# The last 16 attention heads of each layer in pairs: fp32 P times V in the two column halves of TensorE, row sums by adds

## The chip, the cores and the metric

The kernel runs on one core of a Trainium2 chip. Its engines are TensorE (PE; PEld is its weight load), VectorE (DVE), ScalarE (ACT), GpSimd (POOL) and SyncE (SP, which issues nearly all DMAs here). Each takes its own instructions in order, and semaphores hold one engine back until another has done its part. The metric is device microseconds of one execution: before the change 4045.18 us, the median of 3 runs (4043.82 to 4050.78).

## The reference

Two layers of a hybrid block work on 2048 latent tokens behind 256 context tokens, 2304 tokens of width 1024 in all. In each layer a normed and modulated input is projected, and three groups of heads work beside each other: a bidirectional state-space scan (SSD, 6 heads), a bidirectional gated delta rule (GDN, 4 heads) and attention (6 query heads over 2 key-value heads, head width 64). The three outputs are gated, put side by side and projected back. All of it is fp32. For attention the reference does this, in blocks of 128 queries:

```python
q = jnp.moveaxis(q.reshape((Bsz, nb, ATTN_BLOCK) + q.shape[2:]), 1, 0)
s = jnp.einsum('bqhgd,bkhd->bhgqk', qi, k) * scale          # 64 ** -0.5
pr = jax.nn.softmax(s, axis=-1)
o = jnp.einsum('bhgqk,bkhd->bqhgd', pr, v)
```

The latent queries see all 2304 keys; the context queries see the 256 context keys, and only in the first layer.

## The kernel before, in words

A layer goes through three stages: projection of all tokens (lines 370 to 490), then attention together with the SSD and GDN work, and then the output projection (`project`, line 1236).

Attention of the latent tokens is cut into 24 units a layer: 4 blocks of 512 queries times 6 heads. A unit has two parts. `unit_max` (line 521) finds the row maxima: 16 products of 512 keys and 4 of 256 (`pq`, line 536), each reduced by VectorE (`mx`, line 538), and then puts the negated maxima into row 64 of the tile `qm`. `unit_main` (line 550) goes over the 18 tiles of 128 keys (a "key tile" below). For each it makes transposed scores with two products in the fast fp32r form (`pst`, lines 567 and 568), takes the exponential on ScalarE into `pe` (line 570) and accumulates V transposed times P in `po` (line 561). V has a column of ones beside its 64 columns, so `po` has 65 rows, and one of them is the row sum.

In the first 13 units line 561 is one fp32 product of `pe` with `v1`. In the other 11 it is three fp32r products: ScalarE rounds `pe` to `ph` (line 575), VectorE makes the rest `pl` (line 576), V was split once into `vh[0]` and `vh[1]` (lines 658 and 659), and `vh[0]` by `ph`, `vh[1]` by `ph` and `vh[0]` by `pl` are summed in `po`. The function `adv` spreads the maxima of the next unit over the key tiles of this one. PSUM has three score slots (`ps_s`), one `po`, and four more banks, of which SSD has three and attention one (`banks(1, 3)`) until GDN takes all four (`banks(0, 4)`).

Beside these units, and in the same queues of the engines, run in this order: the GDN preparation, the SSD states (line 794: products in the column halves of TensorE, since `bn` has 64 columns a group), the SSD outputs (`ssd_out`, one token tile after the other, `py` in line 861 is its product a tile), and then `gdn_chain`: 36 steps a layer, each needing the state `Sc` of the one before. A step begins with 8 products of line 1105 and ends with line 1132. The chain can begin only when `ssd_out` is through, as it takes over its PSUM banks and its SBUF.

The program is written in this order: GDN preparation, SSD, the first 8 units, `gdn_chain`, the other units. A scheduler then sets each engine's order, with that order and `tc.high_priority()` as priorities; the engines keep to its order at run time.

Of the kernel before, what the change touches and what calls it, by code (L numbers as in the profile page):

```python
# [34 lines left out]
GT = 768  # L35

# [48 lines left out]
def hybrid_kernel(ctx, tc, x, c, ctx_in, c_ctx, norm_w, w_mod, b_mod, w_in, conv_w, conv_b, ssd_A_log,  # L85
# [158 lines left out]
    for l in range(DEPTH):  # L244
# [246 lines left out]
        with ExitStack() as bx:  # L491
            splx = bx.enter_context(ExitStack())
            ap_ = splx.enter_context(tc.tile_pool(reuse_waits="tile", name="ap", bufs=2))
            spl = splx.enter_context(tc.tile_pool(reuse_waits="tile", name="spl", bufs=2))
            vh = []
# [25 lines left out]
            def unit_max(h, q0, qn, k0t, k1t, st):  # L521
                kvh = h // 3
                q2 = ap_.tile([P, 512], F32R, name="q2", bufs=3)
                qm = ap_.tile([65, 512], F32R, name="qm", bufs=3)
# [25 lines left out]
            def unit_main(h, q0, qn, k0t, k1t, st, sp=()):  # L550
# [5 lines left out]
                def pv():  # L556
                    kt, pe, ph, pl = pend.pop(0)
                    vs = slice(kvh * 64, kvh * 64 + 65)
                    ops = [(v1, pe)] if ph is None else [(vh[0], ph), (vh[1], ph), (vh[0], pl)]
                    for j, (v, p) in enumerate(ops):  # L560
                        nc.tensor.matmul(po[0:65, :qn], v[:, kt, vs], p[:, :qn], start=(kt == k0t and j == 0),  # L561
                                         stop=(kt == k1t - 1 and j == len(ops) - 1))

                for kt in range(k0t, k1t):
# [4 lines left out]
                    pe = ap_.tile([P, 512], F32, name="pe", bufs=4)  # L569
                    nc.scalar.activation(out=pe[:, :qn], in_=pt[:, :qn], func=AF.Exp, scale=0.125)  # L570
                    ph = pl = None
                    if kt in sp:
                        ph = spl.tile([P, 512], F32R, name="ph", bufs=2)
                        pl = spl.tile([P, 512], F32R, name="pl", bufs=2)
                        nc.scalar.copy(out=ph, in_=pe)  # L575
                        nc.vector.tensor_tensor(out=pl, in0=pe, in1=ph.bitcast(F32), op=ALU.subtract)  # L576
                    pend.append((kt, pe, ph, pl))
                    if len(pend) > (3 if sp else 1):
                        pv()
# [7 lines left out]
                nc.sync.dma_start(mx_d[640 + h * 64:704 + h * 64, q0:q0 + qn], os_[ob:ob + 64, :qn])  # L587
                yield
# [39 lines left out]
            def attention():  # L628
                big = [(h, LC + qb * 512, 512, 0, NT) for qb in range(LX // 512) for h in range(HQ)]
                small = [] if last else [(h, 0, LC, 0, TC) for h in range(HQ)]  # L630
                sb, ss_ = [{} for _ in big], [{} for _ in small]
                mb = [unit_max(*un, st) for un, st in zip(big, sb)]
# [21 lines left out]
                for i, un in enumerate(big):  # L654
                    if i == 13:
                        for _ in range(2):
                            vh.append(spl.tile([P, NT, 129], F32R, name=f"vh{len(vh)}", bufs=1))
# [651 lines left out]
```

## Time and profile before

| | |
|---|---|
| median of 3 runs | 4045.18 us |
| the profiled execution | 4047.43 us |
| its span, first to last instruction | 4045.6 us |
| mean granted TensorE clock, share of 2.4 GHz | 0.959 |
| TensorE busy (matmuls) | 3760.3 us, 93% |
| VectorE busy | 2682.6 us, 66% |
| ScalarE busy | 1831.1 us, 45% |
| GpSimd busy | 1342.1 us, 33% |

A matmul's time in the profile runs from its start to its modelled end, and consecutive ones overlap; what a matmul costs in a full queue is the distance between the starts. One fp32 matmul of the program stands in the profile as two records, an fp32r one as one record. A row of the windows view gives for each engine the busy time in that stretch and, in brackets, the number of its instructions, then the granted clock, the busy share of the DMA engines and GB/s.

### The profile page before, as it was taken

How to read it: one execution, taken by the hardware profiler on the slowest of the kernel's cores; microseconds unless marked ns; L12 is line 12 of the kernel's file. 1: busy time of each engine (PE TensorE's matmuls, PEld its weight loads, DVE VectorE, ACT ScalarE, POOL GpSimd, SP SyncE). 2: the span in 40 equal slices, each digit the busy share in tenths (PEclk: the TensorE clock that was granted, in tenths of full speed). 3: DMA queues.
4: the chain of work that ended last, by engine and by line, in shares of the span. 5: the costliest groups of instructions: out<-in, count | busy, mean ns of one | idle time of the engine just before them, and what ended most of it. 6: DMA issues, size and time to landing. Idle time of an engine off the chain costs nothing. (4 is left out here: it accounts for less than half of the span.)

```text
span 4045.6 us, 69921 instructions
## 1 busy us (share of the span) xinstructions
PE 3760.3 (93%) x25546; PEld 2839.3 (70%) x25546; DVE 2682.6 (66%) x5114; ACT 1831.1 (45%) x3782; POOL 1342.1 (33%) x1710
## 2 busy tenths in 40 slices
PE   8999999888999988887999999999889999889789
PEld 5899999554566655565678999995545566656567
DVE  7556473787778866665547664747886887666633
ACT  5343342443466655662224433424334566556510
POOL 5112130585267422233303130303762573112300
PEclk9999999999999989987999999999999999988889
DMA  6343432353312444547653434322443224444354
GB/s 201 100 141 111 133 110 92 107 156 136 103 55 64 90 108 107 127 100 235 206 168 112 152 104 136 112 99 79 145 135 105 58 66 96 104 103 114 91 173 153
DMA packets 554115, 484.38 MB, mean 120 GB/s; under 512 B 133992, under 2 KB 488620, under 8 KB 553772
## 3 DMA queue, kind: packets, MB, share of 16 engines
q1 hardware_dynamic: 511916, 444.51, 37.7%
q10 hardware_dynamic: 41856, 35.40, 2.9%
q8 instruction: 202, 3.31, 0.3%
q14 instruction: 141, 1.16, 0.1%
HBM read 335.59 MB, written 144.18 MB: 119 GB/s over the span
## 5 line engine op out<-in xcount | busy, mean ns | idle before, releaser
L570 ACT ACTIVATE pe<-pst 128x512 f32<-128x512 f32 (+1 forms) x876 | 512.0, 594 | 635.8 <-PE pst L568 602.2
L538 DVE TENSOR_REDUCE mx<-pq 128x1 f32<-128x512 f32 (+1 forms) x972 | 590.4, 626 | 134.8 <-PE pq L536 130.1
L561 PE MATMUL po<-pe,v 128*65 128x512 f32 x960 | 492.4, 602 | 3.9 <-ACT os__12072 L584 3.9
L536 PE MATMUL pq<-khh,q 128*128 128x512 f32 (+1 forms) x972 | 455.5, 499 | 29.8 <-DVE mx L538 25.9
L567 PE MATMUL pst<-q,khh 128*128 128x512 f32 (+1 forms) x876 | 437.5, 500 | 38.5 <-DVE mx L538 36.4
L455 PE MATMUL ps<-hi,wh 128*128 128x384 f32 (+2 forms) x1296 | 441.1, 340 | 0.0
L455 PE MATMUL ps<-lo,wh 128*128 128x384 f32 (+2 forms) x1296 | 441.1, 340 | 0.0
L455 PE MATMUL ps<-hi,wl 128*128 128x384 f32 (+2 forms) x1296 | 441.0, 340 | 0.0
L576 DVE TENSOR_TENSOR pl<-pe,ph 128x512 fp32r<-128x512 f32 x396 | 318.7, 809 | 108.7 <-ACT ph L575 68.9
L401 PE MATMUL ps<-wh,hi 128*128 128x320 f32 (+1 forms) x1120 | 354.4, 318 | 1.6 <-DVE hi L365 1.6
L568 PE MATMUL pst<-qm,klo 65*128 65x512 f32 (+1 forms) x876 | 355.1, 407 | 0.0
L401 PE MATMUL ps<-wh,lo 128*128 128x320 f32 (+1 forms) x1120 | 349.8, 315 | 1.7 <-DVE lo L366 1.7
L401 PE MATMUL ps<-wl,hi 128*128 128x320 f32 (+1 forms) x1120 | 350.4, 314 | 0.0
L536 PEld LDWEIGHTS pq<-khh,q 128*128 128x128 f32 x972 | 187.3, 195 | 185.0 <-issue 70.2
L376 DVE TENSOR_TENSOR wl<-wt,wh 128x1024 fp32r<-128x1024 f32 (+3 forms) x144 | 175.3, 1246 | 167.2 <-ACT wh L375 165.0
L567 PEld LDWEIGHTS pst<-q,khh 128*128 128x128 f32 x876 | 171.1, 195 | 156.8 <-DVE mx L538 64.1
L575 ACT CAST ph<-pe 128x512 fp32r<-128x512 f32 x396 | 243.5, 619 | 81.9 <-PE po L561 34.9
L561 PE MATMUL po<-ph,vh 128*65 128x512 f32 x792 | 270.1, 423 | 0.1
L455 PEld LDWEIGHTS ps<-lo,wh 128*128 128x128 f32 x1296 | 244.0, 188 | 10.3
L455 PEld LDWEIGHTS ps<-hi,wl 128*128 128x128 f32 x1296 | 243.4, 188 | 10.4
L455 PEld LDWEIGHTS ps<-hi,wh 128*128 128x128 f32 x1296 | 243.4, 188 | 10.2
L1236 PE MATMUL psd<-woh,mh 128*128 128x512 f32 x544 | 217.4, 400 | 16.4 <-ACT mh L1227 15.1
(587 smaller groups left out, 8086.9 us busy)
## 6 DMA issues: line engine op xcount, KB each, us to landing
wt<-in_w_in_dram SPq DMA_DIRECT2D x72, 512.0 KB
wmt<-in_w_mod_dram SPq DMA_DIRECT2D x48, 512.0 KB
pre_d<-pre SPq DMA_DIRECT2D x34, 512.0 KB
acv<-pre_d SPq DMA_DIRECT2D x34, 512.0 KB
kqc<-kt_d SPq DMA_DIRECT2D x68, 256.0 KB
acv<-pre_d SPq DMA_DIRECT2D x68, 256.0 KB
wt<-in_w_in_dram SPq DMA_DIRECT2D x24, 668.0 KB
wt<-in_w_in_dram SPq DMA_DIRECT2D x24, 640.0 KB
```

Source lines behind the costliest of these rows:

```text
L376: nc.vector.tensor_tensor(out=wl[:, ks, :], in0=wt, in1=wh[:, ks, :].bitcast(F32), op=ALU.subtract)
L401: nc.tensor.matmul(ps, hh[:, k, a], ww[:, k, :], start=(n == 0), stop=(n == 3 * KD - 1))
L455: nc.tensor.matmul(ps, ww[:, k, m * P:(m + 1) * P], hh[:, k, s0:s0 + sn], start=(n == 0), stop=(n == 3 * KD - 1))
L536: nc.tensor.matmul(pq[:, :n], q2[:, u * P:(u + 1) * P], khh[:, kvh, k0t * P + a:k0t * P + a + n], start=True, stop=True)
L538: nc.vector.tensor_reduce(mx[:, u, i:i + 1], pq[:, :n], axis=AX.X, op=ALU.max)
L561: nc.tensor.matmul(po[0:65, :qn], v[:, kt, vs], p[:, :qn], start=(kt == k0t and j == 0), stop=(kt == k1t - 1 and j == len(ops) - 1))
L567: nc.tensor.matmul(pt[:, :qn], khh[:, kvh, ks], q2[:, :qn], start=True, stop=False)
L568: nc.tensor.matmul(pt[:, :qn], klo[:, kvh, ks], qm[:, :qn], start=False, stop=True)
L570: nc.scalar.activation(out=pe[:, :qn], in_=pt[:, :qn], func=AF.Exp, scale=0.125)
L575: nc.scalar.copy(out=ph, in_=pe)
L576: nc.vector.tensor_tensor(out=pl, in0=pe, in1=ph.bitcast(F32), op=ALU.subtract)
L1236: nc.tensor.matmul(ps, a, w[k][:, n * 512:n * 512 + 512], start=(k == 0 and i == 0), stop=(k == KD - 1 and i == 2))
```

## The change

The first 8 units of a layer stay as units of one head with the single fp32 product. The other 16 become 8 pairs of two heads over the same 512 queries. A pair goes over the 18 key tiles; for each it makes the scores of both heads, two exponentials into the two halves of one `pe` of 128 x 2 x 512, and every second key tile a "visit" of TensorE multiplies two key tiles: four fp32 products with 64 columns of V, head 0 into the rows 0 to 63 of `po` and head 1 into the rows 64 to 127. The column of ones is not used in a pair: the row sums come from adding up the `pe` tiles (128 x 1024 in one add), 12 of the 18 key tiles on VectorE (11 adds, `acc[0]`) and 6 on GpSimd (5 adds, `acc[1]`), and four products with ones at the end of the pair (`pl`, line 637 of the changed kernel). The splits of P and V are gone. There are 6 buffers of `pe`, each twice as large, in place of 4.

```diff
@@ unit_main: the split is gone, one product is left @@
-                    kt, pe, ph, pl = pend.pop(0)
-                    vs = slice(kvh * 64, kvh * 64 + 65)
-                    ops = [(v1, pe)] if ph is None else [(vh[0], ph), (vh[1], ph), (vh[0], pl)]
-                    for j, (v, p) in enumerate(ops):
-                        nc.tensor.matmul(po[0:65, :qn], v[:, kt, vs], p[:, :qn], start=(kt == k0t and j == 0),
-                                         stop=(kt == k1t - 1 and j == len(ops) - 1))
+                    kt, pe = pend.pop(0)
+                    nc.tensor.matmul(po[0:65, :qn], v1[:, kt, kvh * 64:kvh * 64 + 65], pe[:, :qn], start=(kt == k0t), stop=(kt == k1t - 1))
...
@@ new: pair_main @@
+                def visit(n, behind_mm):
+                    with tc.high_priority():
+                        for v in range(n):
+                            kt, pe = pend.pop(0)
+                            for j in range(2):
+                                c0 = kvh[j] * 65
+                                mm = nc.tensor.matmul(po[half[j]], v1[:, kt, c0:c0 + 64], pe[:, j], start=(kt == k0t), stop=(kt == k1t - 1))
+                                if v == 0 and j == 0:
+                                    behind(mm, behind_mm)
+
+                for kt in range(k0t, k1t):
+                    ks = slice(kt * P, (kt + 1) * P)
+                    pe = ap_.tile([P, 2, 512], F32, name="pe", bufs=PB)
+                    for j in range(2):
+                        pt = aslot("pst")
+                        nc.tensor.matmul(pt, khh[:, kvh[j], ks], st["q2"][j], start=True, stop=False)
+                        mm = nc.tensor.matmul(pt, klo[:, kvh[j], ks], st["qm"][j], start=False, stop=True)
+                        nc.scalar.activation(out=pe[:, j], in_=pt, func=AF.Exp, scale=0.125)
+                        if j == 0:
+                            yield
+                    e = int((kt - k0t) % 3 == 1)
+                    eng = (nc.vector, nc.gpsimd)[e]
+                    if e in acc:
+                        eng.tensor_tensor(out=acc[e], in0=acc[e], in1=pe, op=ALU.add)
...
+                    pend.append((kt, pe))
+                    if len(pend) == 3:
+                        visit(2, mm)
+                    yield
+                visit(len(pend), mm)
+                os_ = ap_.tile([P, 512], F32, name="os2", bufs=1)
+                nc.scalar.copy(out=os_, in_=po)
+                pl = aslot("pl")
+                for j in range(2):
+                    for e in range(2):
+                        nc.tensor.matmul(pl[half[j]], cc("ones")[:, 0:64], acc[e][:, j], start=(e == 0), stop=(e == 1))
...
@@ attention(): 8 units, then 8 pairs @@
+                units = [(1, un) for un in big[:NS]] + [(2, un) for un in big[NS::2]]
```

What the scheduler makes of it on TensorE, in the first layer while the GDN chain runs. Before, about unit 18 of 24 (L567 and L568 are the scores, L561 the three products with V, L536 the next unit's maxima, L1105 the first products of a chain step):

```order
L536 MATMUL pq<-khh,q_18102 128x512 x2
L567 MATMUL pst<-q_17807,khh 128x512
L568 MATMUL pst<-qm,klo 128x512
L561 MATMUL po<-pl,vh_16904 65x512
L561 MATMUL po<-ph,vh_16904 65x512
L561 MATMUL po<-ph,vh_16905 65x512
L1105 MATMUL p<-Sc,kqc 64x64 x8
```

After, at a like place (L613 and L614 are the scores, L604 a visit, L1159 the first products of a chain step):

```order
L613 MATMUL pst<-q_17173,khh 128x512
L614 MATMUL pst<-qm,klo 128x512
L536 MATMUL pq<-khh,q_17710 128x512 x2
L1159 MATMUL p<-Sc,kqc 64x64 x8
L1168 MATMUL p<-Sc,kqc 64x64 x2
L613 MATMUL pst<-q_17327,khh 128x512
L614 MATMUL pst<-qm,klo 128x512
L604 MATMUL po<-pe,v_352 64x512 x4
```

Three products of 65 columns a key tile and head have become one of 64, and four of them stand together. Counted over the whole order, the first layer's last score product stands behind 33 steps of the chain before and behind 30 after; in the second layer behind 35 and 30. The first SSD output tile stands at about unit 10.1 before and 9.2 after in the first layer, 34.4 and 33.9 (counting on) in the second. The first chain step of the first layer stands at about unit 15.2 before and 14.4 after.

The end of the first layer's second pair on TensorE after the change (L637 are the products of the two sums `acc` with ones, L613 and L614 the first scores of the next pair, the others SSD):

```order
L604 MATMUL po<-pe,v_352 64x512
L915 MATMUL py<-xn_10157,m_10161 128x64 x3
L637 MATMUL pl<-acc_16474,cst 64x512
L613 MATMUL pst<-q_16423,khh 128x512
L614 MATMUL pst<-qm,klo 128x512
L901 MATMUL po_10286<-S,bc 128x192
L902 MATMUL po_10286<-S,bc 128x192
L637 MATMUL pl<-acc_16520,cst 64x512
```

The first `acc` is VectorE's, the second GpSimd's; the products that wait for them stand in front of SSD products and of the next pair's.

VectorE in the second layer's SSD outputs after the change (L624 and L621 are the adds, L538 the maxima, L898 to L904 SSD):

```order
L899 TENSOR_TENSOR m_29511<-m_29511,ee 128x384
L624 TENSOR_TENSOR acc_36068<-pe 128x1024
L922 TENSOR_SCALAR t_29426<-t_29426,sq 128x384
L904 TENSOR_TENSOR t_29519<-po_29543,ecum 128x192
L904 TENSOR_TENSOR t_29520<-po_29543,ecum 128x192
L538 TENSOR_REDUCE mx<-pq 128x1 x2
L904 TENSOR_TENSOR t_29519<-po_29568,ecum 128x192
```

The adds stand between SSD's work and the maxima, in a part of the program where before the single fp32 product asked nothing of VectorE.

## Rows read from the trace of the kernel before

**Rows 1.** The page's first part: busy us, share of the span, instructions.

```profile
PE 3760.3 (93%) x25546; PEld 2839.3 (70%) x25546; DVE 2682.6 (66%) x5114; ACT 1831.1 (45%) x3782; POOL 1342.1 (33%) x1710
```

**Rows 2.** Windows: stretch, its us, PE, PEld, DVE, ACT, POOL busy, clock, DMA, GB/s.

```profile
1051.00:1126.70 75.70, 74.14 (x316) 40.19 (x315) 60.41 (x117) 36.95 (x82) 20.98 (x22) 1.00 0.25 78
1126.70:1396.40 269.70, 258.44 (x1217) 166.64 (x1216) 223.57 (x440) 180.79 (x466) 168.94 (x180) 0.99 0.27 69
1396.40:1809.40 413.00, 362.45 (x4722) 248.46 (x4721) 271.66 (x462) 246.80 (x476) 104.38 (x88) 0.90 0.48 111
3162.40:3400.00 237.60, 226.68 (x1051) 145.89 (x1051) 193.28 (x381) 153.28 (x398) 145.71 (x157) 0.97 0.25 64
3400.00:3819.70 419.70, 372.61 (x4713) 255.03 (x4713) 278.96 (x467) 253.46 (x489) 100.14 (x86) 0.91 0.47 108
```

**Rows 3.** Windows of line 1105 alone (PE, PEld): 16 records are one chain step.

```profile
1396.40:1809.40 413.00, 27.09 (x528) 21.97 (x528) 0.90 0.48 111
3400.00:3819.70 419.70, 26.91 (x544) 21.79 (x544) 0.91 0.47 108
```

**Rows 4.** Windows of line 567 alone: 18 records are one unit.

```profile
1126.70:1396.40 269.70, 49.11 (x94) 17.72 (x94) 0.99 0.27 69
```

**Rows 5.** Timeline of TensorE, fp32r products in a row: start us, us, engine, line.

```profile
1702.15 0.39 PE L567 MATMUL pst<-q,khh 128*128 128x512 f32 x1
1702.38 0.39 PE L568 MATMUL pst<-qm,klo 65*128 65x512 f32 x1
```

**Rows 6.** Timeline of TensorE, one fp32 product with V, then SSD products in column halves.

```profile
1034.93 1.02 PE L561 MATMUL po<-pe,v 128*65 128x512 f32 x2
1035.39 0.79 PE L536 MATMUL pq<-khh,q 128*128 128x512 f32 x1
1036.02 0.39 PE L567 MATMUL pst<-q,khh 128*128 128x512 f32 x1
1036.25 0.39 PE L568 MATMUL pst<-qm,klo 65*128 65x512 f32 x1
1036.57 0.55 PE L794 MATMUL pst<-xd,bn 128*64 128x192 f32 x4
1037.05 0.66 PE L781 MATMUL pt<-cst,xb 128*128 128x128 f32 x4
```

**Rows 7.** Line 794, all its records: ns min/median/max, first and last start.

```profile
L794 PE MATMUL pst<-xd,bn x288: 326/326/377, 1015.9 to 3121.6; 128*64 128x192 f32 x144
```

**Rows 8.** Two SBUF operands: ns min/median/max; of L376 busy us, mean ns.

```profile
L217 DVE TENSOR_TENSOR wml<-wmt,wmh x24: 1202/2074/3407, 6.7 to 2014.9; 128x1024 fp32r<-128x1024 f32 x24
L217 POOL TENSOR_TENSOR wml<-wmt,wmh x24: 2352/2518/8822, 8.2 to 2013.9; 128x1024 fp32r<-128x1024 f32 x24
L821 DVE SCALAR_TENSOR_TENSOR m<-cst,sp,m x204: 334/342/1114, 1117.4 to 3353.4; 128x128 f32<-128x128 f32 x102
L845 DVE TENSOR_TENSOR m<-m,ee x68: 541/788/1385, 1125.2 to 3374.2; 128x384 f32<-128x384 f32 x68
L376 DVE TENSOR_TENSOR wl<-wt,wh 128x1024 fp32r<-128x1024 f32 x72 | 88.3, 1251 | 77.8 <-ACT wh L375 75.6 <-DMA q<-qt_d 2.2
```

**Rows 9.** VectorE's groups from 1126.7 to 1396.4: busy, mean ns, idle before.

```profile
L821 DVE SCALAR_TENSOR_TENSOR m<-cst,sp,m 128x128 f32<-128x128 f32 x96 | 47.3, 555 | 0.9 <-POOL m L818 0.9
L576 DVE TENSOR_TENSOR pl<-pe,ph 128x512 fp32r<-128x512 f32 x39 | 33.4, 863 | 5.0 <-ACT ph L575 4.9
```

**Rows 10.** TensorE's waits from 1396.4 to 1809.4: us in total, times, longest.

```profile
PE po L561 <- DVE pl L576: 10.0, 3, 3.7
PE pq L536 <- DVE mx L538: 8.6, 4, 2.7
```

**Rows 11.** Timeline of TensorE, the last chain steps of the first layer.

```profile
1809.48 0.68 PE L1105 MATMUL p<-Sc,kqc 64*64 64x64 f32 x16
1815.32 0.68 PE L1105 MATMUL p<-Sc,kqc 64*64 64x64 f32 x16
1819.40 0.68 PE L1105 MATMUL p<-Sc,kqc 64*64 64x64 f32 x16 [0.61 <-DVE Sc L1132]
```

More of the change, by code (lines that the diff above doesn't have):

```diff
@@ L35 @@
 GT = 768
+PB = 6
+NS = 8
 def rev(t):
@@ L587, in unit_main, with pair_max @@
                 nc.sync.dma_start(mx_d[640 + h * 64:704 + h * 64, q0:q0 + qn], os_[ob:ob + 64, :qn])
+                yield
+            def pair_max(h0, q0, qn, k0t, k1t, st):
+                st.update(q2=[], qm=[])
+                gens = []
+                for j in range(2):
+                    sj = {}
+                    g = unit_max(h0 + j, q0, qn, k0t, k1t, sj)
+                    for i, _ in enumerate(g):
+                        if i == 0:
+                            st["q2"].append(sj["q2"])
+                            st["qm"].append(sj["qm"])
+                        yield
@@ L630, in attention @@
                 small = [] if last else [(h, 0, LC, 0, TC) for h in range(HQ)]
-                sb, ss_ = [{} for _ in big], [{} for _ in small]
-                mb = [unit_max(*un, st) for un, st in zip(big, sb)]
+                units = [(1, un) for un in big[:NS]] + [(2, un) for un in big[NS::2]]
+                sb, ss_ = [{} for _ in units], [{} for _ in small]
+                mb = [(unit_max if n == 1 else pair_max)(*un, st) for (n, un), st in zip(units, sb)]
                 ms = [unit_max(*un, st) for un, st in zip(small, ss_)]
@@ L653, in attention @@
                         pass
[L654 to L657, printed above, removed]
-                        nc.scalar.copy(out=vh[0], in_=v1)
-                        nc.vector.tensor_tensor(out=vh[1], in0=v1, in1=vh[0].bitcast(F32), op=ALU.subtract)
-                    spn = () if i < 13 else range(NT)
+                at = 0
+                for i, (n, un) in enumerate(units):
                     nxt = ms[i:i + 1] + mb[i + 1:i + 2]
-                    left = (21 + 3) * (i + 1 < len(big)) + 3 * (i < len(small))
+                    left = (24 * units[i + 1][0] if i + 1 < len(units) else 0) + 6 * (i < len(small))
+                    steps = n * (NT - 4)
                     done = 0
-                    for j, _ in enumerate(unit_main(*un, sb[i], spn)):
-                        want = left * (j + 1) // (NT - 4)
+                    for j, _ in enumerate((unit_main if n == 1 else pair_main)(*un, sb[i])):
+                        want = left * (j + 1) // steps
                         adv(nxt, want - done)
@@ L671, in attention @@
                             pass
-                    if i >= 14:
-                        next(side_work, None)
-                    if i % HQ == HQ - 1:
-                        if small and i == HQ - 1:
+                    at += n
+                    for k in range(at - n, at):
+                        if k >= 14:
+                            next(side_work, None)
+                    if at % HQ == 0:
+                        if small and at == HQ:
                             inv(0, LC)
-                        inv(big[i][1], 512)
+                        inv(un[1], 512)
                     yield
```

38 lines of the change are left out of this document (24 added, 14 removed).

## The prediction

> **What bounds the kernel now.** I read the page's first part first: TensorE is busy for 93% of the span, VectorE for 66%, ScalarE for 45%, GpSimd for 33% [rows 1]. An average over stages says little about one of them, so I cut the attention stage of the first layer into windows [rows 2]. From 1051.0 us (unit 8 done) to 1126.7 (first SSD output) TensorE is busy for 74.1 of 75.7 us. In the SSD outputs, to 1396.4, it is 258.4 of 269.7, but VectorE is at 223.6 (83%) and GpSimd at 168.9. In the GDN chain, to 1809.4, TensorE has 362.5 of 413.0 at a granted clock of 0.90 (elsewhere 0.99 to 1.00), so part of that time ran at 1.2 GHz instead of 2.4, and no other engine is above 66%. The reader is to see three different limits: TensorE; TensorE with VectorE close behind; a serial chain with attention between its steps.
>
> In the chain the row of line 1105 gives the pace: 528 records of 16 a step are 33 steps in 413.0 us, 12.5 us each; in the second layer 544 are 34 in 419.7, 12.3 each [rows 3]. Once attention runs out a step takes 5.0 us: three starts between 1809.48 and 1819.40 [rows 11].
>
> **The prices on TensorE.** Two fp32r products of 512 columns start 0.23 us apart [rows 5]. The fp32 product with V and the maxima's product behind it take 1036.02 - 1034.93 = 1.09 us; less 0.23 that is 0.86, two records of 0.43 [rows 6]. A unit of one head costs, for 16 maxima products at 0.23 and 4 at half that (4.2 us in all) and 18 key tiles, with the fp32 product 18 x (0.46 + 0.86) + 4.2 = 28.0 us, with the split 18 x 5 x 0.23 + 4.2 = 24.9.
>
> Whether two column halves run at once is the question on which the change rests, and line 794 answers it: fp32 products of 64 columns, into the two halves of one bank, with different moving data, as in a visit. Its four records take 0.55 us in all, and one alone takes 0.326 [rows 6, 7], so the last starts 0.22 after the first. At 0.43 x 192 / 512 = 0.16 a record, three one after the other would put it at 0.48. So two run at once. The switch into and out of that form costs: from 1036.25 to 1037.05 are 0.80 us, less 0.23 for line 568 and 2 x 0.16 leaves 0.24. A visit then costs 4 x 0.43 + 0.24 = 1.96 us where the split pays 12 x 0.23 = 2.76 and the fp32 units 4 x 0.86 = 3.44. The products with ones stand with two of one half in a row, so I count 6 x 0.43 + 0.24 = 2.8 a pair. Half a pair is 18 x 0.46 + 4.2 + 9 x 1.96 / 2 + 1.4 = 22.7 us: 5.3 less than a unit with the fp32 product, 2.2 less than a split one. Five of the first and eleven of the second a layer make 51 us, 101 in both layers, if all of it reached the end.
>
> **What reaches it, stage by stage.**
>
> From unit 8 to the SSD outputs TensorE is the limit. By the order the outputs begin at unit 9.2 instead of 10.1, in the second layer 1.9 instead of 2.4 units after the eighth. That is 2.1 x 28.0 - 1.2 x 22.7 = 32 us earlier and 2.4 x 28.0 - 1.9 x 22.7 = 24: -56 us. The SSD states only move ahead of unit 8.
>
> In the SSD outputs VectorE takes over. 94 records are 5.2 units [rows 4], so 2.6 pairs with 28 adds on VectorE and 13 on GpSimd. An add of 128 x 1024 takes 1.25 us by line 376, and 2.07 by line 217, the same shape while GpSimd works too, with extremes of 1.20 and 3.41 [rows 8]. The split `pl` (33.4 us [rows 9]) goes, so VectorE has 223.6 - 33.4 + 28 x 1.25 to 2.07 = 225 to 248 us to do, GpSimd 168.9 + 13 x 2.5 = 202, TensorE about 238. The 20 us that TensorE saves there lie beside VectorE. Line 821 already takes 555 ns on average in this stretch against 334 at its fastest [rows 8, 9]: 96 x 0.22 = 21 us are lost with GpSimd busy for 63%, and 75% makes that about 4 more, as much again for the others. I take 8 us more for the stage, 16 for both layers; the bounds are 25 less (TensorE's pace) and 45 more a layer (every add at 3.41). Behind the adds on VectorE's queue stand the maxima, whose PSUM slots TensorE needs.
>
> The Trainium skill has a rule that weighs on this place: the page SBUF — State Buffer, section Who interferes with whom, says that a VectorE instruction with two SBUF inputs and a GpSimd instruction that reads SBUF exclude each other, and that the one which starts first holds the port for its whole length. The extremes of lines 217 and 821 agree; that it is so for each pair, no row shows. What it would make of the time is a rival below.
>
> In the chain the steps stand further apart in attention: the last scores stand behind 30 steps instead of 33, and 30 instead of 35. A step has 9.6 / 30 x 22.7 = 7.3 us of attention on TensorE in it, before 8.8 / 33 x 24.9 = 6.6; against these 0.7 us stand the waits for `pl` (10.0 us over 33 steps on the matmul side alone [rows 10], about as much on the weight side) and the ScalarE rounding. So I leave a step at 12.5 and 12.3 us and let 3 and 5 steps run alone at 5.0: -3 x 7.5 - 5 x 7.3 = -59 us. Bounds: a step of 11.4 (only TensorE's work, fewer waits) and 13.4 (a GpSimd add of 2.5 in front of what the chain needs from GpSimd, a VectorE add of 2 us in front of its differences), 60 us either way over 60 steps. In front of the chain's products now stand visits of 1.96 us in one piece, where single products of 0.23 stood.
>
> A new wait: at the end of each pair the products with ones wait for the last add, and the next pair's scores and SSD's products stand behind them. One add is 1.25 us; 16 of them are 20 us. The bounds are nothing and 40 (GpSimd's 2.5).
>
> ScalarE loses 11 x 18 roundings a layer, which hide beside TensorE; the loads of `q` and the stores stay as many. The first 8 units and the projections I leave alone.
>
> Sum: -56 + 16 - 59 + 20 = -79 us. The profiled execution took 4047.4 us, so 3968; the median of the runs is 2.2 us lower, so 3966.
>
> **Rivals.**
>
> The port excludes strictly. In the SSD outputs GpSimd's 168.9 and its 32.5 us of adds, VectorE's 28 adds at 1.25 (35 us), 96 of line 821 at 0.334 (32) and 35 of line 845 at 0.541 (19) [rows 8] then stand one behind the other: 287 us, 17 more than the window, 9 more than I take; with the second layer 3984. For it speak the extremes; against it that line 821's median is 342 although GpSimd is busy most of the time.
>
> VectorE keeps up and a step shrinks. The SSD outputs take 20 us less a layer, a step 11.9, the row sums cost nothing: -56 - 40 - 59 - 36 = -191, so about 3855. For it speaks that VectorE and ScalarE lose `pl` and `ph` in the chain; against it the 83% in the SSD outputs, and the chain's serial steps.
>
> Slower: the adds hold up VectorE and GpSimd in order. An add of 3.4 us on VectorE in front of the maxima leaves TensorE without score slots: the SSD outputs take 45 and 40 us more, a step 13.4, the row sums 40 us. -56 + 85 - 59 + 54 + 40 = +64, so 4110. It decides from an average add of 2.7 us on, or a step of 13.2. Line 217's median of 2.07 speaks against it, its 3.41 for it.
>
> The halves don't pair with 512 columns: a visit costs 3.7 us, 15.5 a pair more over nine visits, 248 in all, and the time would be about 4190. Line 794 speaks against it.
>
> **How the numbers follow.** I give my sum 0.40, the strict port 0.14, the keeping up 0.20, slower 0.17, unpaired halves 0.03, and a balance of gain and loss near the time before 0.06. What a measurement of this kernel can tell from no change is about 0.2%, 8 us. My sum's own range is 3930 to 4005. Faster by over 0.2%: 0.73; within it 0.07; slower 0.20. The range reaches half into the case that VectorE keeps up and half into the slower one: 3870 to 4080.
>
> **What would show it.** Two records of the new line 604 starting within 0.02 us of each other and 0.43 from the next two; the first SSD output some 30 us earlier in each layer; VectorE above 90% in the SSD outputs with adds of about 2 us; a step of 12 to 13 us, 30 of them before the last score; waits of about 1 us at line 637. If a step is under 12 us or the SSD window under 255, the gain is larger; if adds average over 2.7 us, it is gone.

## The result and the profile after

The changed kernel takes 4234.44 us (median of 4 runs, 4224.46 to 4254.53) where the kernel before takes 4047.98: 1.0468 times as long, 95% interval 1.0427 to 1.0508. 3966 had been forecast.

The page's first part, and the span with the mean granted clock:

```profile
PE 3853.0 (91%) x25278; PEld 2766.7 (65%) x25278; DVE 2678.2 (63%) x4892; ACT 1599.7 (38%) x3384; POOL 1551.7 (37%) x1790
```
```profile
core 0: 4230.7 us, clock 0.915
```

Most of the answer lies in the span, if one takes it apart. Idle time is the span less TensorE's busy time. The clock stands at one of two levels, 1.2 or 2.4 GHz, and work at 1.2 takes about twice as long (a row below: 3.69 us against 1.94). So what the clock costs is taken as half of the time that TensorE is busy at 1.2 GHz, and busy time less that is the work, as if at full clock. The trace lists both the stretches of half clock and the matmuls. The shorter sum (1 - clock) x span would be 166 and 360 us, but it counts idle time at half clock as lost twice: over the whole span TensorE is busy for 79% of the half-clock time before and 82% after.

| | work, us | idle, us | lost to the clock, us | span, us |
|---|---|---|---|---|
| before | 3628.1 | 285.3 | 132.2 | 4045.6 |
| after | 3558.6 | 377.7 | 294.4 | 4230.7 |
| difference | -69.5 | +92.4 | +162.2 | +185.1 |

The work fell by 70 us, where the prices gave 101. TensorE then stood idle longer, and was at half its clock for twice as long (717 us against 334).

By stage (columns as in [rows 2]; from unit 8 to the first SSD output, the SSD outputs, the chain with attention in it, the chain alone; then the second layer without the first of these):

```profile
1083.60:1141.80 58.20, 47.85 (x148) 21.69 (x146) 55.90 (x87) 23.08 (x52) 21.05 (x16) 0.82 0.10 30
1141.80:1474.30 332.50, 290.95 (x1230) 166.24 (x1229) 255.26 (x434) 160.03 (x429) 207.99 (x193) 0.86 0.22 56
1474.30:1869.80 395.50, 355.05 (x4213) 198.75 (x4206) 211.52 (x317) 152.71 (x310) 145.65 (x98) 0.87 0.49 110
1869.80:1945.30 75.50, 46.55 (x641) 26.02 (x641) 30.34 (x49) 25.59 (x43) 39.73 (x29) 0.63 0.80 214
3277.60:3574.80 297.20, 269.99 (x1090) 158.36 (x1090) 222.29 (x388) 141.01 (x376) 184.38 (x171) 0.82 0.20 52
3574.80:3967.50 392.70, 354.47 (x4117) 198.59 (x4110) 217.72 (x312) 149.71 (x306) 141.49 (x94) 0.87 0.47 110
3967.50:4024.30 56.80, 27.77 (x571) 19.62 (x571) 20.22 (x38) 12.91 (x29) 27.09 (x24) 0.63 0.49 124
```

Against [rows 2] the SSD outputs take 332.5 instead of 269.7 us and 297.2 instead of 237.6, with clocks of 0.86 and 0.82 instead of 0.99 and 0.97: +122 us, of which 47 are idle time of TensorE and 85 the clock, while its work there is 10 less. VectorE is busy for 77 and 75% of them, less than the 83 and 81% of before: no engine is full. The chain with its tail takes 471.0 and 449.5 us instead of 423.4 and 428.0: +69. The rest is small and cancels (the first scores 13.5 us later in the first layer, -10 between the layers and -11 after the chain).

Line 1159 alone, as in [rows 3] (480 records are 30 steps; 96 are 6):

```profile
1474.30:1869.80 395.50, 23.52 (x480) 18.91 (x480) 0.87 0.49 110
3574.80:3967.50 392.70, 21.97 (x480) 17.56 (x480) 0.87 0.47 110
3967.50:4024.30 56.80, 5.57 (x96) 4.73 (x96) 0.63 0.49 124
```

So 30 steps stand beside attention in both layers, as forecast, at 13.2 and 13.1 us each. The other 6 take 9.5 to 12.6 us each, not 5.0.

Where TensorE waits in the first layer, from unit 8 to the end of the SSD outputs: us in total, times, longest; first after, then before.

```profile
PE pq L536 <- DVE mx L538: 15.1, 11, 3.1
PE pst L613 <- DVE mx L538: 13.9, 9, 2.6
```
```profile
PE pq L536 <- DVE mx L538: 3.3, 7, 1.2
PE pst L567 <- DVE mx L538: 2.6, 5, 0.7
```

It waits five times as long for VectorE's maxima (29.0 us against 5.9; in the second layer's SSD outputs 13.6 against 4.5). A wait for another result of VectorE shows what follows, in slices of 6 us (columns as above), with TensorE's rows there:

```profile
1176.00:1182.00 6.00, 6.00 (x30) 3.54 (x28) 2.53 (x4) 4.41 (x13) 6.00 (x5) 1.00 0.61 191
1182.00:1188.00 6.00, 2.43 (x8) 0.81 (x6) 6.00 (x10) 2.35 (x7) 3.58 (x4) 0.85 0.31 98
1188.00:1194.00 6.00, 5.77 (x20) 2.66 (x20) 4.03 (x8) 1.43 (x3) 3.67 (x4) 0.58 0.01 3
1194.00:1200.00 6.00, 6.00 (x31) 4.21 (x30) 4.08 (x6) 4.61 (x16) 4.97 (x6) 1.00 0.31 89
```
```profile
1183.36 1.07 PE L604 MATMUL po<-pe,v 128*64 128x512 f32 x2
1188.23 3.69 PE L637 MATMUL pl<-acc,cst 128*64 128x512 f32 x8 [3.80 <-DVE acc L621]
1191.84 0.80 PE L613 MATMUL pst<-q,khh 128*128 128x512 f32 x1
```

TensorE stands idle for 3.8 us, waiting for an add on VectorE, which is busy for all 6 us of that slice. The add comes late because each queue is worked off in order:

```profile
1176.28 3.36 POOL L621 TENSOR_TENSOR acc<-acc,pe 128x1024 f32<-128x1024 f32 x1
1180.37 1.48 POOL L872 TENSOR_TENSOR m<-cst,sp 128x768 f32<-128x768 f32 x1
1181.89 0.90 DVE L875 SCALAR_TENSOR_TENSOR m<-cst,sp,m 128x128 f32<-128x128 f32 x1 [2.78 <-POOL m L872]
1186.96 1.21 DVE L621 TENSOR_TENSOR acc<-acc,pe 128x1024 f32<-128x1024 f32 x1
```

GpSimd's add of 3.36 us stands in front of SSD's `m` (line 872), VectorE waits 2.78 us for that `m`, and VectorE's own add stands behind. When TensorE goes on the clock is at half, and the eight products with ones take 3.69 us; eight records of the same shape take 1.94 us at full clock:

```profile
1109.25 1.94 PE L604 MATMUL po<-pe,v 128*64 128x512 f32 x8
```

So the wait is paid twice, once as idle time and once in the work behind it. The Trainium skill (TensorE: Matmul & The Clock Gate, section What's actually happening) says that the throttled state is the default and that activity releases it; these slices agree, with 1.00 before the wait, 0.58 after it, and 1.00 again once TensorE has been busy.

The last row also settles the pairing of the column halves: at 0.43 us a record one after the other, eight would need 3.4.

### The profile page after: what moved, and what is told of

Same layout as the page of the kernel before. It is cut to its first block, busy times and chain, and to the rows that moved or that the text cites. A ratio compares the mean times of both kernels' runs of the same rounds, so it can differ in the third digit from the quotient of the medians.

```text
span 4230.7 us, 68193 instructions
## 1 busy us (share of the span) xinstructions
PE 3853.0 (91%) x25278; PEld 2766.7 (65%) x25278; DVE 2678.2 (63%) x4892; ACT 1599.7 (38%) x3384; POOL 1551.7 (37%) x1790
## 5 line engine op out<-in xcount | busy, mean ns | idle before, releaser
L538 DVE TENSOR_REDUCE mx<-pq 128x1 f32<-128x512 f32 (+1 forms) x972 | 581.9, 625 | 225.0 <-PE pq L536 222.4
L615 ACT ACTIVATE pe<-pst 128x512 f32<-128x512 f32 x576 | 333.3, 596 | 541.5 <-PE pst L614 537.7
L536 PE MATMUL pq<-khh,q 128*128 128x512 f32 (+1 forms) x972 | 453.0, 511 | 88.1 <-DVE mx L538 70.4
L536 PEld LDWEIGHTS pq<-khh,q 128*128 128x128 f32 x972 | 194.4, 208 | 296.8 <-DVE mx L538 130.7
L604 PE MATMUL po<-pe,v 128*64 128x512 f32 x1152 | 365.0, 723 | 1.6 <-ACT pe L615 1.5
L613 PE MATMUL pst<-q,khh 128*128 128x512 f32 x576 | 288.4, 501 | 32.9 <-DVE mx L538 20.8
L558 PE MATMUL po<-pe,v 128*65 128x512 f32 x600 | 306.2, 602 | 2.0 <-ACT os__11415 L574 0.8
L566 ACT ACTIVATE pe<-pst 128x512 f32<-128x512 f32 x300 | 172.8, 589 | 298.5 <-PE pst L564 296.8
L621 DVE TENSOR_TENSOR acc<-acc,pe 128x1024 f32<-128x1024 f32 x160 | 222.8, 1392 | 84.4 <-ACT pe L615 83.6
L614 PE MATMUL pst<-qm,klo 65*128 65x512 f32 x576 | 252.5, 438 | 0.0
L1290 PE MATMUL psd<-woh,ml 128*128 128x512 f32 x544 | 216.3, 398 | 0.3
```

Source lines behind the costliest of these rows:

```text
L536: nc.tensor.matmul(pq[:, :n], q2[:, u * P:(u + 1) * P], khh[:, kvh, k0t * P + a:k0t * P + a + n], start=True, stop=True)
L538: nc.vector.tensor_reduce(mx[:, u, i:i + 1], pq[:, :n], axis=AX.X, op=ALU.max)
L558: nc.tensor.matmul(po[0:65, :qn], v1[:, kt, kvh * 64:kvh * 64 + 65], pe[:, :qn], start=(kt == k0t), stop=(kt == k1t - 1))
L604: mm = nc.tensor.matmul(po[half[j]], v1[:, kt, c0:c0 + 64], pe[:, j], start=(kt == k0t), stop=(kt == k1t - 1))
L613: nc.tensor.matmul(pt, khh[:, kvh[j], ks], st["q2"][j], start=True, stop=False)
L614: mm = nc.tensor.matmul(pt, klo[:, kvh[j], ks], st["qm"][j], start=False, stop=True)
```

## The experiments

Theory A: the adds hold up VectorE and GpSimd in order. B, later D: the pairs' form, with visits in one piece. C: a unit with less work on TensorE only makes TensorE wait for the maxima, and its clock falls. In the table work, idle time and clock loss are of the profiled execution, split as above, in us; medians and ratios (to the kernel before, with the 95% interval) are of all runs. The kernel before was measured again beside each group of runs (medians 4037 to 4046 us), so two runs of different groups are better compared by their ratios.

| run | median us | ratio | work | idle | clock loss |
|---|---|---|---|---|---|
| e1 no adds | 4138 | 1.0219 [1.0185, 1.0252] | 3555 | 332 | 250 |
| e2 no adds on GpSimd | 4167 | 1.0297 [1.0264, 1.0330] | 3547 | 341 | 291 |
| e3 adds on VectorE | 4207 | 1.0412 [1.0373, 1.0451] | 3546 | 364 | 301 |
| e4 singles | 4050 | 1.0016 [1.0003, 1.0030] | 3699 | 244 | 116 |
| e5 spread | 4216 | 1.0439 [1.0417, 1.0461] | 3538 | 385 | 289 |
| e6 pairs from unit 17 | 4088 | 1.0112 [1.0093, 1.0132] | 3609 | 281 | 192 |
| e7 visits of one key tile | 4253 | 1.0529 [1.0502, 1.0556] | 3589 | 372 | 283 |
| e8 both heads in one half | 4352 | 1.0768 [1.0746, 1.0790] | 3767 | 310 | 275 |
| e9 singles, 65 columns | 4010 | 0.9926 [0.9913, 0.9938] | 3692 | 224 | 85 |
| e10 singles, 64 columns | 4125 | 1.0207 [1.0194, 1.0221] | 3921 | 151 | 56 |
| e11 singles, 128 columns | 4009 | 0.9930 [0.9912, 0.9948] | 3697 | 224 | 75 |
| e12 own pool | 4228 | 1.0468 [1.0454, 1.0482] | 3551 | 403 | 265 |
| e13 thin singles | 3888 | 0.9599 [0.9575, 0.9623] | 3169 | 437 | 290 |
| e14 single visits | 4055 | 1.0019 [1.0002, 1.0036] | 3737 | 220 | 81 |
| e15 no priority | 4231 | 1.0448 [1.0426, 1.0470] | 3559 | 379 | 292 |
| e16 64 columns, pieces of 2 | 4118 | 1.0199 [1.0172, 1.0226] | 3879 | 169 | 68 |
| e17 64 columns, pieces of 4 | 4317 | 1.0684 [1.0652, 1.0715] | 3829 | 284 | 214 |
| e18 65 columns, pieces of 4 | 4259 | 1.0533 [1.0504, 1.0561] | 3724 | 306 | 234 |

**The adds: e1 to e3.** e1 has `pass` for the later adds and ones for the row sums; e2 leaves out GpSimd's alone; e3 puts all on VectorE:

```diff
                     if e in acc:
-                        eng.tensor_tensor(out=acc[e], in0=acc[e], in1=pe, op=ALU.add)
+                        pass
...
-                nc.scalar.copy(out=sm_, in_=pl[0:65])
+                nc.scalar.activation(out=sm_, in_=pl[0:65], func=AF.Exp, scale=0.0)
```
```diff
-                    eng = (nc.vector, nc.gpsimd)[e]
+                    eng = nc.vector
```

> Leaves out 14 of the 16 adds of a pair (the first one on VectorE and the first one on GpSimd stay, so that the products with ones have their operands) and writes ones in place of the row sums; the products, the exponentials, the visits and the stores stay. Theory A, the adds: they stand in order in front of the maxima on VectorE and in front of SSD's operations on GpSimd, TensorE waits for the maxima and its clock is halved after each wait. Then most of the 187 us that the change costs comes back: 4060 us or less, half-clock time from 719 us to under 450, SSD outputs at 15 us a tile or less. Theory B, the pairs themselves (visits in one piece, one accumulator bank for two heads, the end of a pair): the time stays above 4170, with the clock as low.

> Leaves out the 4 later adds of a pair on GpSimd (2.3 to 3.4 us each) and writes ones in place of the row sums; the adds on VectorE stay. If within theory A it is GpSimd's adds (in front of the operation of line 872, for which VectorE and then the maxima wait), this alone gives back over 100 us, to 4130 or less. If it is VectorE's adds, under 40 us: above 4190. Theory B: under 20.

> All 16 adds of a pair on VectorE. If GpSimd's adds are what hurts: 4150 or less. If VectorE's place in front of the maxima is what hurts: 4 more adds of 1.4 us a pair on 16 pairs, 90 us of VectorE work, 4270 or more. Theory B: within 20 us of 4234.

All three fell between their bounds. The adds are worth 96 us, about half of the loss; GpSimd's alone 67 of them. On VectorE instead of GpSimd they cost 27 us less (23 by the ratios, and the runs of the two kernels overlap), though VectorE is then busy for 48 us more. The SSD outputs without adds:

```profile
1133.30:1430.00 296.70, 272.45 (x1209) 158.49 (x1207) 201.79 (x400) 158.21 (x427) 168.43 (x181) 0.90 0.25 64
3216.70:3484.10 267.40, 250.47 (x1099) 147.53 (x1099) 177.23 (x357) 142.21 (x382) 147.62 (x161) 0.89 0.22 61
```

36 and 30 us shorter, still 27 and 30 longer than before the change. The chain to its end does not gain: 478.1 and 444.8 us. In the first layer's SSD outputs TensorE still waits 14.4 us for maxima. The other half of the loss is not the adds.

**Singles: e4, and pairs from unit 17 on: e6.** `NS = 24` and `NS = 16` for `NS = 8`.

> All 24 units as units of one head with the fp32 product (no pairs, no column halves, no adds, and no fp32r split either). By the prices on TensorE, 3.1 us more for each of the 11 units a layer that were split: 68 us, 4116 us, with the clock as before the change (0.96). If the pairs are to blame for the low clock, it comes out below the changed kernel's 4234. If instead the taking away of the split, with its even TensorE load, is to blame, the clock is 0.92 here too and the time 4200 or more.

> Pairs for the last 8 units only; units 9 to 16 are units of one head with the fp32 product. Theory C: the SSD outputs run as with single units (no half clock there, 14 us a tile), which takes away 100 us of idle time and halved clock a layer and adds 8 x 5.3 = 42 of TensorE work: about 4120. Theory D: the loss goes with the number of visits, half of 184 us stays: about 4142, and the SSD outputs of single units beside no visit don't explain more. If the loss of the change sat in the chain alone, 4200 or more.

e4 is the surprise: with 71 us more work on TensorE than before the change it takes as long, since idle time and clock give back 58 in the profiled execution (the slowest of its ten runs). Without the split VectorE is busy for 297 us less and ScalarE for 228, and since attention now outlasts the chain by some 90 us a layer, no step stands alone. In e6 the SSD outputs (of both layers), then the chain:

```profile
1124.90:1384.10 259.20, 250.09 (x1142) 156.59 (x1141) 189.37 (x393) 153.60 (x415) 165.64 (x180) 0.99 0.26 68
3181.30:3408.70 227.40, 221.19 (x991) 138.89 (x991) 167.37 (x349) 135.57 (x366) 142.68 (x157) 1.00 0.25 67
```
```profile
1384.10:1845.20 461.10, 407.96 (x4856) 234.35 (x4855) 239.60 (x377) 169.44 (x346) 161.16 (x113) 0.86 0.47 107
3408.70:3865.80 457.10, 409.00 (x4755) 232.68 (x4755) 234.92 (x371) 167.23 (x340) 155.19 (x109) 0.85 0.44 105
```

Without pairs the SSD outputs run at full clock and take 10 us a layer less than before the change: the loss there is the pairs'. The chain keeps the low clock, 0.86 and 0.85. Both theories had expected more time, 4120 and 4142 us.

**Is TensorE's work worth its price? e8 and e13.** e8 sends both heads into one half; e13 is e9 (below) with an fp32r product:

```diff
-  nc.tensor.matmul(po[half[j]], v1[...], pe[:, j], ...)
+  nc.tensor.matmul(po[half[j if kt == k0t else 0]], v1[...], pe[:, j], ...)
```
```diff
+            nc.scalar.copy(out=v1r, in_=v1)
...
-  nc.tensor.matmul(po[0:65, :qn], v1[...], pe[:, :qn], ...)
+  nc.tensor.matmul(po[0:65, :qn], v1r[...], pe[:, :qn], ...)
```

> From the second key tile on, both heads' products with V go into the same column half of the accumulator (the second head's sum is wrong for it), so that they can't run at once: 17 x 0.86 = 15 us more of TensorE work a pair, 234 us in all; everything else stays. Theory C: the work falls into the waits for VectorE and keeps the clock up: less than half of it shows, below 4350, with less than 719 us of half clock. Theory D: TensorE is what bounds and all of it shows: 4450 to 4480.

> Single units as in the 65-column run (4010 us), but the product with V in one fp32r product of 0.23 us instead of the fp32 one of 0.86 (the low parts of the exponentials and of V are left out): 18 x 0.63 = 11.4 us of TensorE work less a unit, 547 us in all, with no pairs, no visits, no column halves and no adds. Theory C, TensorE's work is on the path only where no other engine is: the units ahead of the SSD outputs give back 8.5 x 11.4 = 97 us a layer, the rest of attention behind the chain at most 70 a layer; the SSD outputs stay at 200 us or more and a chain step at 11.5 us or more, with more idle time and half-clock time over 400 us (195 there): 3700 to 3830, less than half of the 547. Theory G, it is the pairs' form that brings waits and low clock, and TensorE's work is worth its price: 3463 to 3600, half-clock time under 250 us.

In e8 209 us more work cost 118, just past what C allowed (4350). In e13 524 us less work (against e9) gave 122 (132 by the ratios), less than even C had allowed; idle time rose by 212 and the clock's loss by 205. Its SSD outputs, then those of e9, then its chain of the second layer beside attention and alone:

```profile
1094.00:1369.50 275.50, 250.54 (x1166) 172.38 (x1164) 206.44 (x420) 168.58 (x447) 164.89 (x180) 0.92 0.26 68
3058.10:3307.30 249.20, 226.63 (x1037) 157.17 (x1035) 181.69 (x369) 148.55 (x394) 143.49 (x157) 0.89 0.25 63
```
```profile
1077.80:1338.00 260.20, 250.31 (x1152) 157.31 (x1151) 191.57 (x395) 155.20 (x419) 163.85 (x179) 1.00 0.26 68
3092.20:3321.50 229.30, 222.40 (x1031) 139.93 (x1029) 165.24 (x345) 137.30 (x371) 143.00 (x158) 1.00 0.26 69
```
```profile
3307.30:3534.80 227.50, 198.78 (x2549) 139.65 (x2548) 92.19 (x165) 95.26 (x193) 40.97 (x39) 0.81 0.50 109
3534.80:3690.20 155.40, 78.15 (x1694) 65.47 (x1694) 44.03 (x92) 32.62 (x76) 63.57 (x54) 0.51 0.60 136
```

With neither pairs nor adds nor column halves the clock falls to 0.92 and 0.89 in the SSD outputs, and they get longer than e9's. More attention lies in them (6.3 and 5.6 units against 4.9 and 4.4), but TensorE's work in them is still 21 and 22 us less; in the first layer's it waits 11.7 us for maxima, against 5.7 in e9. Theory G falls; what C says of waits and clock holds there, while its time (3700 to 3830) was missed. e13 is faster than both kernels, but it leaves out the low parts of the exponentials and of V.

**How the pairs are issued: e5, e7, e15.** The steps of the maxima over 34 half steps; visits of one key tile; no priority:

```diff
-                    steps = n * (NT - 4)
+                    steps = n * (NT - 4) if n == 1 else 2 * NT - 2
```
```diff
-                    if len(pend) == 3:
-                        visit(2, mm)
+                    if len(pend) == 2:
+                        visit(1, mm)
```
```diff
-                    with tc.high_priority():
+                    if True:
```

> The 48 steps of the next pair's maxima are spread over 34 of a pair's 36 half steps instead of 28. Theory C, coupling and clock: the pairs take less of TensorE as priced, but so the maxima come too thick for VectorE, TensorE waits a microsecond or more for them and its clock is halved after it. Then fewer waits before lines 536 and 613 and less half-clock time than 719 us: 4205 or less. Theory D, the visits: products in one piece in front of SSD's and the chain's; how the maxima are spread changes nothing, 4234 within 15.

> A visit has one key tile instead of two: 18 pieces of 1.1 us a pair where 9 of 1.96 stood, 0.24 us more for each switch, 35 us of TensorE work in all. Theory D: shorter pieces let SSD's and the chain's products in earlier: 4190 or less. Theory C: the length of a piece matters little, 4220 to 4270.

> The changed kernel without putting the visits ahead: the scheduler places them by their order in the program. Theory D: SSD's and the chain's products come earlier, 4200 or less. Theory C: 4234 within 15.

Spreading gave 19 us by the medians and 12 by the ratios, and its runs overlap with those of the changed kernel: it decides nothing between C (30) and D (15). Priority is worth nothing. Visits of one key tile cost 19 us (25 by the ratios) with 31 us more work; what they gave back is within the noise, and it is not what D wanted.

**The place of the first maxima: e9 and e12.** e9 is e4 with smaller tiles, e12 the changed kernel with the pairs' tiles in a pool of their own:

```diff
-  pe = ap_.tile([P, 2, 512], F32, name="pe", bufs=PB)[:, 0]
+  pe = ap_.tile([P, 512], F32, name="pe1", bufs=4)
```
```diff
+  pp = splx.enter_context(tc.tile_pool(reuse_waits="tile", name="pp", bufs=1))
...
-  pe = ap_.tile([P, 2, 512], F32, name="pe", bufs=PB)
+  pe = pp.tile([P, 2, 512], F32, name="pe", bufs=PB)
```

> Single units only (as the run of singles, 4050 us), but their exponentials in tiles of 512 columns, four of them, instead of six of 1024. Then the first unit's maxima stand beside the projections again, as before the change, instead of behind the last of them: its first scores come 13.5 us earlier in the first layer and 20 in the second, 4017 us. If that place of the maxima doesn't matter, 4050 within 8.

> The changed kernel with the pairs' tiles (exponentials, sums, results) in a memory pool of their own, opened after the one of the single units. The first unit's maxima stand beside the projections again. If 33 us of the loss are that, 4200 us; if not, 4234 within 10. The rest of the loss stays: half-clock time above 650 us.

e9 gained 41 us on e4 (36 by the ratios; 33 expected). e12 gained nothing, though its scores did start 15 us earlier in the first layer and 20 in the second (counted from the chain's end before it). Another order of the queues ate the gain: 10.7 units of scores now stand before the first SSD output instead of 9.9 and 10.0, which comes 22 and 8 us later after the first score, and the first layer's SSD outputs take 11 us more. Attention now ended 25 and 27 steps into the chain instead of 30, but that made the two chains only 20 us shorter in all. The second layer's chain, beside attention and alone, and what TensorE waited for in the second stretch:

```profile
3582.90:3916.30 333.40, 303.40 (x3595) 169.45 (x3594) 181.77 (x263) 128.74 (x263) 119.01 (x79) 0.89 0.45 106
3916.30:4008.40 92.10, 45.64 (x1005) 35.33 (x1005) 31.03 (x60) 21.19 (x49) 41.55 (x35) 0.61 0.53 127
```
```profile
PE pv L1127 <- DMA acv<-pre_d: 27.9, 6, 12.2
PE p L1183 <- ACT Vc L1179: 7.3, 5, 4.5
```

Nine steps alone take 10 us each: for 28 of their 92 us TensorE waits for the chain's own loads, and the clock is 0.61. A step without attention costs only 1 to 2 us less there than one with it, in both layers.

**Why the chain's clock stays low: e10, e11, e14, e16 to e18.** All are e9 with another product with V. Width:

```diff
-  po[0:65, :qn], v1[:, kt, kvh * 64:kvh * 64 + 65]
+  po[0:64, :qn], v1[:, kt, kvh * 65:kvh * 65 + 64]
```
```diff
-  po[0:65, :qn], v1[:, kt, kvh * 64:kvh * 64 + 65]
+  po[:, :qn], v1[:, kt, kvh:kvh + P]
```

> As the run before it in this list, but the fp32 product with V takes 64 columns of TensorE (one column half, always the same) instead of 65, with as many products in the same order; ones are written in place of the row sums. Theory E, width: after a fall the clock stays low for longer where the products with V are in a column half, so the half-clock stretches in the chain get longer (about 9 us each instead of 4.4) and the half-clock time rises by over 80 us: 30 us or more slower than its 65-column twin. Theory F, waits alone: as long as TensorE waits as often, the clock is the same: within 8 us of its twin.

> As the 65-column twin, but the product with V takes all 128 columns (both heads' V and the ones; the rows that are not wanted are not stored), with as many products in the same order. Theory E: the half-clock stretches in the chain get shorter than 4.4 us, the time is 5 to 20 us below its twin. Theory F: within 8 us of its twin.

E fell, and so did the time that F gave for 64 columns. That form costs 115 us, at a higher clock: 229 us more work over 864 products of 512 columns, 0.27 each, near the 0.24 that the prediction took for the switch.

Pieces, as e18 has them (e16 and e17 are the same with 64 columns, e16 with 2 for 4; e14 has 2, 65 columns and no `behind`):

```diff
                 def pv():
-                    kt, pe = pend.pop(0)
-                    nc.tensor.matmul(po[0:65, :qn], ...)
+                  for i in range(min(4, len(pend))):
+                    kt, pe = pend.pop(0)
+                    p_ = nc.tensor.matmul(po[0:65, :qn], ...)
+                    if i == 0:
+                        behind(p_, mm)
...
-                    if len(pend) > 1:
-                        pv()
+                    if len(pend) > 4:
+                        with tc.high_priority():
+                            pv()
```

> Single units as in the 65-column run (4010 us), with the fp32 products with V of two key tiles in one piece, put ahead as the visits are. The TensorE work is the same. Theory D, visits: pieces in front of the chain's serial products make its steps longer (from 12.2 and 11.4 us to 13) and the half-clock stretches in it longer (from 4.9 us to 8 or more): 4040 or more. Theory C: the pieces cost nothing by themselves, 4010 within 12.

> The 64-column single units (4125 us, 61 us of half clock in the chains of both layers), with the products with V of two key tiles held back until the second's score is out and so mostly issued in one piece of 1.96 us, as long as a visit of the pairs. Ones in place of the row sums. Theory H, narrow pieces: products in 64 columns issued in a piece keep the clock low after a fall, and that is why the chain of the pairs has 260 to 290 us of half clock: over 150 us here. Theory I, the piece is nothing to the clock: under 90 us; the switch is paid once for two products, 4020 to 4080 us.

> The same with four key tiles in a piece (3.7 us, six tiles for the exponentials instead of four), as long as the visits of the run with both heads in one half, which had 260 us of half clock in its chains. Theory H: over 200 us of half clock in the chains. Theory I: under 90.

> The 65-column single units with four key tiles in a piece of 3.4 us, the same but for the width. If H holds and width matters, under 100 us of half clock in the chains; if any long piece does it, over 200 here too; by Theory I under 90, and 4010 to 4060 us.

e14 says nothing about pieces: in its trace the products mostly stand one at a time. Its 45 us (38 by the ratios) are 44 of work that I can't place. e16, with nearly two thirds of its products in pieces, has 81 us of half clock in the chains, little more than the 61 of e10. e17 has 231 us, e18 267. The chain of e9, then that of e18:

```profile
1338.00:1777.50 439.50, 394.41 (x4795) 228.63 (x4796) 182.68 (x343) 164.25 (x333) 104.67 (x93) 0.95 0.48 108
3321.50:3732.90 411.40, 375.23 (x4615) 219.81 (x4609) 172.43 (x327) 155.06 (x316) 100.10 (x89) 0.95 0.47 110
```
```profile
1379.10:1874.70 495.60, 443.71 (x4811) 252.84 (x4811) 185.52 (x347) 165.10 (x335) 105.80 (x93) 0.87 0.44 96
3514.80:4005.10 490.30, 442.06 (x4647) 254.00 (x4647) 182.82 (x339) 163.78 (x332) 97.29 (x88) 0.86 0.40 92
```

With 31 us more work e18 is 249 us slower than e9 (245 by the ratios), nearly all of it clock and idle time (its six tiles also put the first maxima behind the projections, as in e4, which was 41 us slower than e9). So it isn't the width: pieces of four, held back until the fifth score, can do it in single units. Whether the pairs' visits of two key tiles are long enough stays open: e16's pieces, as long, did not do it, and shorter visits (e7) hardly helped.

## Why the prediction was wrong

**The prices on TensorE were near.** The halves pair, with 1.94 us for eight records (1.96 forecast). The work fell by 70 us of the 101; why the rest is missing is not shown. e7's visits cost 31 us of work (35 expected), unpaired halves 209 (234 expected; in that rival 3966 and 248 make 4214, not 4190). What failed is how they were turned into time: every term was made at full clock, and a gap was counted at its own length alone.

**From unit 8 to the SSD outputs: -56 forecast, +2 measured** (from the first score to the first output 417.8 and 424.2 us before, 419.3 and 424.8 after). By units the forecast held (9.2, and 2.0 after the eighth in the second layer). TensorE's work up to the first output fell by 17 and 12 us, and its idle time and clock took 18 and 12 back: "TensorE is the limit" did not survive the first pair, where VectorE is busy for 55.9 of 58.2 us, at a clock of 0.82 instead of 1.00. And "the first 8 units and the projections I leave alone" failed: the larger tiles put the first unit's maxima behind the last projection. e12 shows that mending this alone buys nothing.

**The SSD outputs: "I take 8 us more for the stage", 63 and 60 measured.** This is the step that failed most, past its own bound of 45. It added up VectorE's work and found that it fits; it does fit (75 to 77%). But VectorE's queue is in order, its SSD operations wait for GpSimd's and TensorE's, and the maxima wait behind them. Before the change TensorE had 0.86 us of product with V a key tile to bridge that, with the pairs 0.49 a head. Of 122 us the adds are 66 (e1); the other 57 go with the pairs, as longer waits for the maxima and a lower clock. e13 shows such waits without any pair and e6 shows them gone with single units, so too little work on TensorE is the likely cause. It is not shown that nothing else of the pairs' form adds to it.

**The adds.** Forecast at about 2 us on VectorE and 2.5 on GpSimd; ns min/median/max:

```profile
L621 DVE TENSOR_TENSOR acc<-acc,pe x160: 1206/1225/2301, 1098.3 to 3972.1; 128x1024 f32<-128x1024 f32 x160
L621 POOL TENSOR_TENSOR acc<-acc,pe x64: 2344/2368/3420, 1114.4 to 3969.4; 128x1024 f32<-128x1024 f32 x64
L875 DVE SCALAR_TENSOR_TENSOR m<-cst,sp,m x204: 334/904/2483, 1123.1 to 3531.4; 128x128 f32<-128x128 f32 x102
```

They were cheap: half of VectorE's took no longer than 1.23 us, 1.39 on average. So the rival "slower" (4110 us) had the right side and, for half of the loss, the right mechanism, but a wrong sign to tell it by, an average add of 2.7 us; its other sign, a step of 13.2 us, was just met. The adds' own length says little about their cost: 64 of 2.4 us on GpSimd, which was idle 63% of the time, cost 67 us (e2).

They cost by their place in the queues, as the rows at 1176 us show, and the rival of the strict port has a part in it that these runs do not separate from the place. SSD's operation with two SBUF operands has a median of 904 ns (line 875; line 821 before the change: 342 [rows 8]), and without GpSimd's later adds 342 again (e2). VectorE's adds took 1.62 us on average where GpSimd was at work for over 80% of their time (46 of them), 1.22 where for under 20% (96). The port rule of the Trainium skill (SBUF — State Buffer, Who interferes with whom) agrees with these rows. Measured against the shortest of each kind, line 875 lost 31 us more than before the change in both layers together, VectorE's adds 30 us and GpSimd's 10. How much of this reached the end of the program is not shown.

**The chain: -59 forecast, +69 measured.** 30 steps beside attention came as forecast. A step takes 13.2 instead of 12.5 us, within the bounds (44 us of the gap of 128). "Let 3 and 5 steps run alone at 5.0" failed: that pace was read from the last steps before, at full clock and hardly waiting; six steps a layer alone take 12.6 and 9.5 (72 us), at a clock of 0.63, with waits for loads and for the chain's own results on VectorE and ScalarE. The term offered a gain where there was none: a step without attention is not 7.5 but 0.6 to 3.6 us shorter than one with it, so taking attention out of steps frees little.

**The row sums: 20 forecast**; the products with ones waited 17.2 us for adds in six places. Right in size, but behind the longest of these waits the clock fell as well. At full clock the eight records of a pair took 1.94 us, not 2.8.

What stays open: why the pairs hold the clock at 0.86 in the chain where single units have 0.95, with and without the adds, in one piece or two. Their chain is 20 to 50 us longer than that of e9 with less work in it. Beside attention the clock does not fall more often than before the change (23 times in both layers, against 27) and TensorE is idle for less (79 us against 98), but it stays at half for 8 to 9 us at a time instead of 6; in e9 for 4 to 5, in e18 for 8.

## What to carry to other kernels

Before taking work off TensorE, look at what it bridges: where another engine's in-order queue feeds it, work taken away turns into waits, and the clock makes each wait cost more than its length. Take work, idle time and clock apart first, and don't count idle time at half clock as lost to the clock. A version with more TensorE work and less for VectorE and ScalarE (e9 and e11, singles without split) beats both kernels here, the one before by 0.7%. And don't read the pace of a chain that is left alone from its last two or three steps: with six to nine of them alone, loads and a low clock made it twice as slow.

## What was unexpected of the hardware

The clock's cost doubled (132 to 294 us). From 1083 to 1474 us of the changed kernel the granted clock fell 16 times, 15 of them during an idle stretch of TensorE of 1.2 to 3.8 us or within 2.3 us after one. fp32 products issued four in a row raised that cost from 85 to 234 us with 31 us more work (e9 to e18). Products of 64 columns between full-width ones cost 0.27 us more than those of 65 or 128, which cost the same (4010 and 4009 us).
